# TensorE held to the program's order while a token mixing runs, side steps behind whole units of big products

## The chip, the cores and the metric

One core of a Trainium2 chip runs the whole kernel. The metric is device time in microseconds (us) of one launch; the kernel before takes 1155.15 us, the median of 3 runs (1153.23 to 1157.84).

## The reference, cut to what matters

One layer on 528 tokens (16 meta tokens and 512 frames) of width 1024:

```
h += 0.5 * swiglu(rmsnorm(h))                    # FFN 1, inner width 2816
z  = rmsnorm(h) @ w_in                           # 2464 columns
h += concat(rwkv7(z[:, :1696]), attention(z[:, 1696:])) @ w_out
h += 0.5 * swiglu(rmsnorm(h))                    # FFN 2
out = rmsnorm(h)[16:]
# rwkv7: 8 heads of 64, a recurrence over the tokens
#   S = S*w_t + (S @ -kk_t) (kk_t*a_t)^T + v_t k_t^T ;  y_t = S r_t
# attention: 8 query and 2 key heads, chunks of 64 frames, a window of 3 chunks,
#   the meta tokens and a sink
```

## The kernel before

Tokens run along the free axis in two halves: half 0 has 272 (16 meta tokens and 256 frames), half 1 has 256. A *unit* is one 128-column tile of a weight matrix with 8 blocks of 128 rows: `prep` loads 512 KB through SyncE's queue (L120), ScalarE casts them to the high half `whi` (L122), VectorE subtracts to get the low half `wlo` (L125), and TensorE does 24 matmuls of 128 x 272 or 128 x 256 (high by high, high by low, low by high: L199, L200, L195, and L208 in the down projections). `raw`, `whi` and `wlo` have three buffers each, and units are prepared three ahead. A unit's accumulator (tile `big`, four PSUM banks) is then evicted by VectorE and ScalarE.

`drive` (L131) traces the units of a list in order; after each it calls `advance` (L166), which gives every running side chain the unit's cost as credit (2.72 for half 0, 2.56 for half 1). A side chain is a Python generator: it traces one step, yields what the step costs, and is called again while its credit is positive. The list (L1032 to L1040): four units of half 1's FFN 1; the 14 units of half 0's input projection that feed RWKV, with elementwise work and small matmuls behind each (`on_z`; the last small matmul of each of four head pairs is L561); `begin`, which starts the RWKV chain; the 6 units of attention's projection; `begin_at`, which starts the attention chain; the other 62 units of half 1's FFN 1; `end`, which joins the chains; 8 units of output projection (`w_out`). Then the same for half 1's mixing, with 6 + 56 units of half 0's FFN 2 as cover.

The RWKV chain: `tinv` sends gram tiles through DRAM (L681 and L685, on ScalarE's queue), VectorE inverts 80 triangular 32 x 32 blocks in 31 dependent pairs of operations (L694, L696; phase `tik`), the result goes back through DRAM (L702 to L714), and 64 + 64 matmuls of 32 x 32 finish it (L721, L729; phase `tizo`). `chain` then goes through 5 chunks (4 in half 1), each in steps: X and Z (L781, L784), the solve (L796), values of the next chunk (L759, L764), state and output (L806 to L816), and a group norm with one matmul (L840). These matmuls write the tile `mx`, two PSUM banks. Attention goes through 4 chunks, each a transposition of V (L868), and twice: scores (L878), softmax, transposition (L898), product (L910).

The trace order isn't the order on the chip: at compile time a scheduler models the engines and puts on each the instruction that is ready first, the earlier traced first among those; `high_priority` moves the RWKV steps ahead (100 for `chain`, 0 for `tik`). So big products traced later can stand ahead of a small matmul that waits for its data.

Of the kernel before, what the change touches and what calls it, by code (L numbers as in the profile page):

```python
# [32 lines left out]
BRIDGE = 4  # L33
WO = (4, 5, 6, 7, 0, 1, 2, 3)
WARM = 12
TIW, CHW, ATW = 1.4, 0.55, 0.9
NK = D // 128


# [26 lines left out]
NU = len(UNIT)  # L66


class Prog:
    def __init__(self, ctx, tc, io):  # L70
        self.tc, self.nc, self.io = tc, tc.nc, io
        self.A, self.V, self.P, self.PE = tc.nc.scalar, tc.nc.vector, tc.nc.gpsimd, tc.nc.tensor
        self.uid = 0
        pool = lambda name, **k: ctx.enter_context(tc.tile_pool(name=name, bufs=1, **k))
        self.cst = pool("cst")
        self.rp = pool("res")
        self.np_ = pool("npl")
# [88 lines left out]
    def advance(self, cost):  # L166
        for sd in list(self.sides):
            if sd not in self.sides:
                continue
            sd[1] += cost  # L170
            while sd[1] > 0:
                self.mark(self.ph or sd[2] if sd[2] == 'rwkv' else sd[2])
                with self.tc.high_priority(PRIO.get(self.ph if sd[2] == "rwkv" else "", PRIO[sd[2]])):
                    c = next(sd[0], None)
                if c is None:
                    self.sides.remove(sd)
                    break
                sd[1] -= c

# [492 lines left out]
    def tinv(self, hf, mp, tip):  # L672
# [40 lines left out]
            nc.scalar.dma_start(out=T1c[hr[h]].rearrange("s p c t -> s (p c) t"), in_=d3[g].rearrange("g s t -> s g t"))  # L713
            nc.scalar.dma_start(out=T2c[hr[h]].rearrange("s p c t -> s (p c) t"), in_=d2[1, g].rearrange("g s t -> s g t"))  # L714
        self.ph = 'tizo'
        yield 6.0
        pc = [(p, c, slice((p * 4 + c - 1) * 32, (p * 4 + c) * 32)) for p in range(4) for c in range(1, 5)]
        bz = self.mbank()
        for p, c, o in pc:
# [2 lines left out]
        Z = t(tip, [128, 512], "Z")  # L722
        for h in range(2):
            (A.copy, V.tensor_copy)[h](out=Z[hr[h]], in_=bz[hr[h]])
        yield 2.0
        bo = self.mbank()
        for p, c, o in pc:
            for h in range(2):
# [1 line left out]
        for h in range(2):  # L730
            (A.copy, V.tensor_copy)[h](out=GT[hr[h], 4 * h:4 * h + 4, 1:5, 32:64],
                                       in_=bo[hr[h]].rearrange("p (h s t) -> p h s t", h=4, s=4))
        yield 2.0

    def chain(self, hf, st, mo, cp):

# [32 lines left out]
            pre[n] = (UV, BT)  # L769

        values(0)
        yield CHW
        hp = [(p, h) for p in range(4) for h in range(2)]
        for n, (slot, tok, C) in enumerate(chunks):
            self.ph = f'ch{slot}'
            ur, vr = (slice(0, C), slice(64, 64 + C)), (slice(64, 64 + C), slice(0, C))
            gt = lambda rows, h, p, c: GT[rows[h], 4 * h + p, slot, c:c + C]
            UV, BT = pre.pop(n)
            X, Z = self.mbank(), self.mbank() if slot else None
            for p, h in hp:  # L780
                PE.matmul(X[ur[h], cols(p)], gt(vr, h, p, 0), UV[vr[h], h, p], start=True, stop=True)  # L781
            if slot:
                for p, h in hp:
                    PE.matmul(Z[hs[h], cols(p)], self.AR[p][hs[h], slot, 0:64], S[hs[h], p], start=True, stop=True)  # L784
            Rs = t(cp, [128, 256], "Rs")
            if slot:
                A.copy(out=Rs, in_=X[:, 0:256])
                V.tensor_tensor(out=Rs, in0=Z[:, 0:256], in1=Rs, op=ALU.add)
            else:
                for h in range(2):  # L790
                    A.copy(out=Rs[ur[h]], in_=X[ur[h], 0:256])
            step()
            yield 2 * CHW
            X = self.mbank()
            for p, h in hp:
                PE.matmul(X[ur[h], cols(p)], gt(ur, h, p, 0), Rs[ur[h], cols(p)], start=True, stop=True)  # L796
            for h in range(2):
                (A.copy, V.tensor_copy)[h](out=UV[ur[h], h], in_=X[ur[h], 0:256].rearrange("p (j c) -> p j c", j=4))
            step()
            yield CHW  # L800
            if n + 1 < len(chunks):
                values(n + 1)
            yield CHW
            X, Z = self.mbank(), self.mbank()
            for p, h in hp:
                PE.matmul(Z[hs[h], cols(p)], BT[vr[h], h, p], UV[vr[h], h, p], start=True, stop=True)  # L806
                PE.matmul(X[hs[h], cols(p)], BT[ur[h], h, p], UV[ur[h], h, p], start=True, stop=True)
            if slot:
                for p in range(4):
                    for h in range(2):  # L810
                        PE.matmul(X[hs[h], cols(p, 256)], S[hs[h], p], self.AR[p][hs[h], slot, 64:64 + C],
                                  start=True, stop=False)
                    for h in range(2):
                        PE.matmul(Z[hs[h], cols(p, 256)], UV[vr[h], h, p], gt(vr, h, p, 64), start=True, stop=True)
                    for h in range(2):
                        PE.matmul(X[hs[h], cols(p, 256)], UV[ur[h], h, p], gt(ur, h, p, 64), start=False, stop=True)  # L816
            p4 = lambda b, c: b[:, c:c + 256].rearrange("p (j c) -> p j c", j=4)
            for b in (Z, X):
                V.tensor_tensor(out=S, in0=p4(b, 0), in1=S, op=ALU.add)
            V.tensor_tensor(out=S, in0=S, in1=st["ee"][:, :, slot].unsqueeze(2).broadcast_to([128, 4, 64]), op=ALU.mult)  # L820
            if slot:
                Y = t(cp, [128, 4, 64], "Y", bufs=2)
                A.copy(out=Y, in_=p4(Z, 256))
                V.tensor_tensor(out=Y, in0=p4(X, 256), in1=Y, op=ALU.add)
                norms.append(self.group_norm(st, mo, cp, Y, slice(64 * slot - 64, 64 * slot)))
            step()
            yield 2 * CHW
        self.ph = 'gn'
        while norms:
            step()  # L830
            yield 2.0

    def group_norm(self, st, mo, cp, Y, ts):

# [18 lines left out]
    def attention(self, hf, st, mo, ap_):  # L853
        A, V, P, PE, t = self.A, self.V, self.P, self.PE, self.t
        for ci in range(4):
# [14 lines left out]
                PE.transpose(b[0:W - 81, 128:256], VC[:, 81:W], self.ident)  # L870
                A.copy(out=VK[0:W - 81, 1], in_=b[0:W - 81, 128:256])
            A.copy(out=VK[0:81, 0], in_=b[0:81, 0:128])
            yield ATW
            kss = (slice(0, 64), slice(64, 128))
            for mp2 in range(2):
                bs, rows = self.banks(), []
# [3 lines left out]
                for kv in range(2):  # L880
# [6 lines left out]
                                           scalar=-3e38, op0=ALU.add, op1=ALU.max, accum_out=m[:, 1:2])  # L887
                    V.tensor_scalar(out=m[:, 2:3], in0=m[:, 0:1], scalar1=m[:, 1:2], scalar2=-1.0, op0=ALU.max, op1=ALU.mult)
                    rows.append((s, m))
                yield ATW  # L890
                for s, m in rows:
                    A.activation(s[:, 0:W], s[:, 0:W], AF.Exp, bias=m[:, 2:3], accum_out=m[:, 3:4])
                yield ATW
                b, bo = self.banks()
                for kv, (s, m) in enumerate(rows):
                    V.reciprocal(m[:, 3:4], m[:, 3:4])
                    A.activation(s[:, 0:W], s[:, 0:W], AF.Copy, scale=m[:, 3:4])
                    PE.transpose(b[0:81, 256 * kv:256 * kv + 128], s[:, 0:81], self.ident)  # L898
                    if nw > 1:
                        PE.transpose(b[0:W - 81, 256 * kv + 128:256 * kv + 256], s[:, 81:W], self.ident)  # L900
                yield ATW
                pTs = []
                for kv in range(2):
                    pT = t(ap_, [128, 2, 128], "pT", bufs=2)
# [6 lines left out]
                if nw > 1:  # L911
                    for kv, ks in enumerate(kss):
                        PE.matmul(bo[ks, 0:128], VK[0:W - 81, 1, ks], pTs[kv][0:W - 81, 1], start=False, stop=True)
                yield ATW
                ms, ts = slice(2 * mp2, 2 * mp2 + 2), slice(64 * ci, 64 * ci + 64)
                ov = bo[:, 0:128].rearrange("p (m t) -> p m t", m=2)
                mh, ml = mo[1][:, ms, 0, ts], mo[1][:, ms, 1, ts]
                A.copy(out=mh, in_=ov)
                V.tensor_tensor(out=ml, in0=ov, in1=mh.bitcast(F32), op=ALU.subtract)
                yield ATW  # L920


def program(tc, io, out):
    with ExitStack() as ctx:
# [37 lines left out]
        def pclose(name):  # L962
            pools.pop(name)[0].__exit__(None, None, None)
# [11 lines left out]
        def mixing(hf):  # L975
            st, mo = {}, []

            def on_z():
                return pr.on_z(hf, st, pools["mix"][1], pools["ew"][1] if "ew" in pools else None)

            def begin_ew():
                popen("ew")

            def rwkv():
                yield from pr.tinv(hf, pools["mix"][1], popen("ti"))
                pclose("ti")
                cp = popen("ch")
                yield from pr.chain(hf, st, mo, cp)
                pclose("ch")

            def begin():
                pclose("ew")
                popen("at")
                mo.extend(pr.operands(hf, 256))
                pr.side(rwkv(), "rwkv")

            def begin_at():
                pr.side(pr.attention(hf, st, mo, pools["at"][1]), "attn")

            def end():  # L1000
                pr.join()
                pclose("at")
            return on_z, act(begin_ew), act(begin), act(begin_at), act(end), mo

# [32 lines left out]
        k = 10  # L1037
# [131 lines left out]
```

## Time and profile before

| | before |
|---|---|
| median of 3 runs | 1155.15 us |
| the profiled execution | 1155.86 us |
| its span, first to last instruction | 1154.0 us |
| TensorE busy | 1113.4 us (96%), 10149 matmuls |
| VectorE busy | 801.7 us (69%) |
| ScalarE busy | 661.8 us (57%) |
| mean granted TensorE clock | 0.976 |

The rows quoted below are from that one execution. An engine is busy while it executes an instruction; a matmul's end is modelled, so TensorE counts as busy also where matmuls follow each other at half the clock. The profile names engines PE (TensorE), DVE (VectorE), ACT (ScalarE), POOL (GpSimd), SP (SyncE); L12 is line 12.

### The profile page before, as it was taken

How to read it: one execution, taken by the hardware profiler on the slowest of the kernel's cores; microseconds unless marked ns; L12 is line 12 of the kernel's file. 1: busy time of each engine (PE TensorE's matmuls, PEld its weight loads, DVE VectorE, ACT ScalarE, POOL GpSimd, SP SyncE). 2: the span in 40 equal slices, each digit the busy share in tenths (PEclk: the TensorE clock that was granted, in tenths of full speed). 3: DMA queues.
4: the chain of work that ended last, by engine and by line, in shares of the span. 5: the costliest groups of instructions: out<-in, count | busy, mean ns of one | idle time of the engine just before them, and what ended most of it. 6: DMA issues, size and time to landing. Idle time of an engine off the chain costs nothing.

```text
span 1154.0 us, 24751 instructions
## 1 busy us (share of the span) xinstructions
PE 1113.4 (96%) x10149; PEld 1065.9 (92%) x10149; DVE 801.7 (69%) x1465; ACT 661.8 (57%) x1118; POOL 37.3 (3%) x91
## 2 busy tenths in 40 slices
PE   8999999999999998999899999997999899999996
PEld 7999999998999997899899898987889899999996
DVE  7866566776778993356888777995356686655555
ACT  7544444686757646565568685574456476444343
POOL 0000000021000000000001000000000000000000
PEclk8999999999999999899999999998899899999998
DMA  7565555545445555223255345456223456665662
GB/s 270 173 184 184 189 175 177 171 133 160 129 130 186 163 169 148 74 95 114 92 184 177 128 142 174 149 163 168 75 82 121 117 166 203 199 207 182 187 185 74
DMA packets 68724, 178.87 MB, mean 155 GB/s; under 512 B 21620, under 2 KB 26868, under 8 KB 68612
## 3 DMA queue, kind: packets, MB, share of 16 engines
q1 hardware_dynamic: 52384, 173.70, 47.9%
q10 hardware_dynamic: 16228, 3.61, 1.5%
q8 instruction: 79, 1.29, 0.5%
q14 instruction: 33, 0.27, 0.1%
HBM read 173.54 MB, written 3.74 MB: 154 GB/s over the span
## 4 chain that ended last, share of the span: by engine, by line
PE 79%; DVE 11%; ACT 3%; DMA 3%; issue 2%; ACTq 1%; DVEq 0%; SPq 0%
PE big L200 23%; PE big L199 23%; PE big L195 16%; PE big L208 6%; DVE wlo L125 4%; DVE tmp L694 3%; DVE rn L696 2%; PE mx L764 1%; ACT whi L122 1%; PE mx L759 1%; DMA raw<-w_in 1%; DMA d<-rn 1%; PE as L878 1%; PE mx L806 1%; PE mx L796 1%
## 5 line engine op out<-in xcount | busy, mean ns | idle before, releaser
L122 ACT CAST whi<-raw 128x1024 fp32r<-128x1024 f32 (+1 forms) x321 | 334.9, 1045 | 283.3 <-PE big L200 205.5
L125 DVE TENSOR_TENSOR wlo<-raw,whi 128x1024 fp32r<-128x1024 f32 x320 | 389.5, 1218 | 105.6 <-ACT whi L122 82.7
L200 PE MATMUL big<-h,whi 128*128 128x256 f32 (+1 forms) x704 | 177.0, 286 | 0.0
L199 PE MATMUL big<-h,whi 128*128 128x256 f32 (+1 forms) x704 | 173.2, 285 | 0.0
L200 PEld LDWEIGHTS big<-h,whi 128*128 128x128 f32 x704 | 133.1, 190 | 1.5 <-issue 0.9
L199 PEld LDWEIGHTS big<-h,whi 128*128 128x128 f32 x704 | 132.3, 190 | 0.6 <-issue 0.3
L199 PE MATMUL big<-n1a,whi 128*128 128x256 f32 x464 | 121.0, 292 | 8.9 <-ACT n1a L849 4.2
L199 PE MATMUL big<-n0a,whi 128*128 128x272 f32 (+1 forms) x464 | 122.3, 293 | 6.4 <-ACT n0a L849 3.2
L200 PE MATMUL big<-n0a,whi 128*128 128x272 f32 (+1 forms) x464 | 121.5, 290 | 0.6 <-DVE n0a L328 0.6
L199 PE MATMUL big<-n0b,whi 128*128 128x272 f32 (+1 forms) x464 | 120.7, 291 | 0.7 <-ACT n0b L327 0.7
L200 PE MATMUL big<-n0b,whi 128*128 128x272 f32 (+1 forms) x464 | 120.1, 288 | 0.4 <-DVE n0b L328 0.4
L200 PE MATMUL big<-n1b,whi 128*128 128x256 f32 x464 | 119.9, 289 | 0.0
L200 PE MATMUL big<-n1a,whi 128*128 128x256 f32 x464 | 119.8, 288 | 0.0
L199 PE MATMUL big<-n1b,whi 128*128 128x256 f32 x464 | 119.3, 288 | 0.0
L208 PE MATMUL big<-h,wlo 128*128 128x256 f32 (+1 forms) x704 | 106.1, 286 | 0.0
L199 PEld LDWEIGHTS big<-n1a,whi 128*128 128x128 f32 x464 | 90.5, 195 | 11.6 <-ACT n1a L849 4.6
L199 PEld LDWEIGHTS big<-n0a,whi 128*128 128x128 f32 x464 | 88.2, 191 | 9.0 <-ACT n0a L849 3.4
L208 PEld LDWEIGHTS big<-h,wlo 128*128 128x128 f32 x704 | 93.8, 190 | 1.1 <-issue 0.6
L200 PEld LDWEIGHTS big<-n1a,whi 128*128 128x128 f32 x464 | 90.5, 195 | 0.7 <-issue 0.3
L200 PEld LDWEIGHTS big<-n1b,whi 128*128 128x128 f32 x464 | 90.0, 194 | 1.2 <-issue 0.2
L199 PEld LDWEIGHTS big<-n1b,whi 128*128 128x128 f32 x464 | 89.8, 194 | 1.3 <-issue 0.8
L200 PEld LDWEIGHTS big<-n0a,whi 128*128 128x128 f32 x464 | 88.4, 191 | 2.5 <-DVE n0a L328 1.0
(294 smaller groups left out, 2032.2 us busy)
## 6 DMA issues: line engine op xcount, KB each, us to landing
raw<-w_in SPq DMA_DIRECT2D x319, 512.0 KB, 3.7
outT<-o SPq DMA_DIRECT2D x8, 256.0 KB, 2.2
res<-xT_in SPq DMA_DIRECT2D x2, 544.0 KB, 4.3
res<-xT_in SPq DMA_DIRECT2D x2, 512.0 KB, 8.6
d<-GT ACTq DMA_DIRECT2D x8, 80.0 KB, 3.6
zk<-d ACTq DMA_DIRECT2D x2, 320.0 KB, 5.1
d<-rn ACTq DMA_DIRECT2D x2, 320.0 KB, 3.6
GT<-d ACTq DMA_DIRECT2D x8, 80.0 KB, 5.8
```

The lines of the kernel that those rows point to most:

```text
L122: self.A.copy(out=hi[:, a:a + n], in_=raw[:, a:a + n])
L125: self.V.tensor_tensor(out=lo[:, 0:nk], in0=raw[:, 0:nk], in1=hi[:, 0:nk].bitcast(F32), op=ALU.subtract)
L195: self.PE.matmul(o, lo[:, k], x(k)[:, 0], start=False, stop=(k == ks[-1]))
L199: self.PE.matmul(o, w, x[:, 0], start=first, stop=False)
L200: self.PE.matmul(o, w, x[:, 1], start=False, stop=False)
L208: self.PE.matmul(o, lo[:, i], x(k)[:, 0], start=False, stop=(k == nk - 1))
L694: V.tensor_tensor(out=m, in0=NT[:n2, 0:k, k].unsqueeze(1).broadcast_to([n2, k, k]), in1=TI[:n2, 0:k, 0:k], op=ALU.mult)
L696: V.tensor_reduce(out=TI[:n2, 0:k, k], in_=m, op=ALU.add, axis=mybir.AxisListType.X)
L759: PE.matmul(b[vr[h], cols(p)], st["vT", p][hs[h], tok:tok + C], self.cent[hs[h], hs[h]], start=True, stop=True)
L764: PE.matmul(b[hs[r], cols(p, 256)], self.BK[p][hs[h], slot, hs[r ^ h]], self.ident[hs[h], hs[h]], start=True, stop=True)
L796: PE.matmul(X[ur[h], cols(p)], gt(ur, h, p, 0), Rs[ur[h], cols(p)], start=True, stop=True)
L806: PE.matmul(Z[hs[h], cols(p)], BT[vr[h], h, p], UV[vr[h], h, p], start=True, stop=True)
```

## The change

The chains no longer yield costs (but for `tik`, whose yields stay): they yield `UNIT_END`, at which `advance` sets their credit to zero and stops, so that one step of each chain is traced behind each whole unit. TensorE is wrapped (`Pinned`); from `begin` to `end` each matmul and transposition gets an order edge to the instruction traced before it on TensorE, which the scheduler must keep. The wait of 6.0 ahead of `tizo` becomes four empty steps. X and Z are traced alternately, `values` comes into the same step as the solve, attention's reciprocal and scaling move up to the exponential, with one empty step behind them. No matmul is added or removed, and no DMA.

```diff
@@ -33,7 +33,9 @@
 BRIDGE = 4
 WO = (4, 5, 6, 7, 0, 1, 2, 3)
 WARM = 12
-TIW, CHW, ATW = 1.4, 0.55, 0.9
+TIW = 1.4
+
+UNIT_END = -1.0
 NK = D // 128
 
 
@@ -66,10 +68,28 @@
 NU = len(UNIT)
 
 
+class Pinned:
+
+
+    def __init__(self, tc, pe):
+        self.tc, self.pe, self.on = tc, pe, False
+
+    def matmul(self, *a, **k):
+        return self.pin(self.pe.matmul(*a, **k))
+
+    def transpose(self, *a, **k):
+        return self.pin(self.pe.transpose(*a, **k))
+
+    def pin(self, ins):
+        if self.on:
+            self.tc.keep_in_program_order(ins)
+        return ins
+
+
 class Prog:
     def __init__(self, ctx, tc, io):
         self.tc, self.nc, self.io = tc, tc.nc, io
-        self.A, self.V, self.P, self.PE = tc.nc.scalar, tc.nc.vector, tc.nc.gpsimd, tc.nc.tensor
+        self.A, self.V, self.P, self.PE = tc.nc.scalar, tc.nc.vector, tc.nc.gpsimd, Pinned(tc, tc.nc.tensor)
         self.uid = 0
         pool = lambda name, **k: ctx.enter_context(tc.tile_pool(name=name, bufs=1, **k))
         self.cst = pool("cst")
@@ -174,6 +194,9 @@
                     c = next(sd[0], None)
                 if c is None:
                     self.sides.remove(sd)
+                    break
+                if c == UNIT_END:
+                    sd[1] = 0.0
                     break
                 sd[1] -= c
 
@@ -713,7 +736,8 @@
             nc.scalar.dma_start(out=T1c[hr[h]].rearrange("s p c t -> s (p c) t"), in_=d3[g].rearrange("g s t -> s g t"))
             nc.scalar.dma_start(out=T2c[hr[h]].rearrange("s p c t -> s (p c) t"), in_=d2[1, g].rearrange("g s t -> s g t"))
         self.ph = 'tizo'
-        yield 6.0
+        for _ in range(4):
+            yield UNIT_END
         pc = [(p, c, slice((p * 4 + c - 1) * 32, (p * 4 + c) * 32)) for p in range(4) for c in range(1, 5)]
         bz = self.mbank()
         for p, c, o in pc:
@@ -779,8 +803,7 @@
             X, Z = self.mbank(), self.mbank() if slot else None
             for p, h in hp:
                 PE.matmul(X[ur[h], cols(p)], gt(vr, h, p, 0), UV[vr[h], h, p], start=True, stop=True)
-            if slot:
-                for p, h in hp:
+                if slot:
                     PE.matmul(Z[hs[h], cols(p)], self.AR[p][hs[h], slot, 0:64], S[hs[h], p], start=True, stop=True)
             Rs = t(cp, [128, 256], "Rs")
             if slot:
@@ -790,17 +813,16 @@
                 for h in range(2):
                     A.copy(out=Rs[ur[h]], in_=X[ur[h], 0:256])
             step()
-            yield 2 * CHW
+            yield UNIT_END
             X = self.mbank()
             for p, h in hp:
                 PE.matmul(X[ur[h], cols(p)], gt(ur, h, p, 0), Rs[ur[h], cols(p)], start=True, stop=True)
             for h in range(2):
                 (A.copy, V.tensor_copy)[h](out=UV[ur[h], h], in_=X[ur[h], 0:256].rearrange("p (j c) -> p j c", j=4))
-            step()
-            yield CHW
             if n + 1 < len(chunks):
                 values(n + 1)
-            yield CHW
+            step()
+            yield UNIT_END
             X, Z = self.mbank(), self.mbank()
             for p, h in hp:
                 PE.matmul(Z[hs[h], cols(p)], BT[vr[h], h, p], UV[vr[h], h, p], start=True, stop=True)
@@ -824,11 +846,11 @@
                 V.tensor_tensor(out=Y, in0=p4(X, 256), in1=Y, op=ALU.add)
                 norms.append(self.group_norm(st, mo, cp, Y, slice(64 * slot - 64, 64 * slot)))
             step()
-            yield 2 * CHW
+            yield UNIT_END
         self.ph = 'gn'
         while norms:
             step()
-            yield 2.0
+            yield UNIT_END
 
     def group_norm(self, st, mo, cp, Y, ts):
 
@@ -887,18 +909,19 @@
                                            scalar=-3e38, op0=ALU.add, op1=ALU.max, accum_out=m[:, 1:2])
                     V.tensor_scalar(out=m[:, 2:3], in0=m[:, 0:1], scalar1=m[:, 1:2], scalar2=-1.0, op0=ALU.max, op1=ALU.mult)
                     rows.append((s, m))
-                yield ATW
                 for s, m in rows:
                     A.activation(s[:, 0:W], s[:, 0:W], AF.Exp, bias=m[:, 2:3], accum_out=m[:, 3:4])
-                yield ATW
+                for s, m in rows:
+                    V.reciprocal(m[:, 3:4], m[:, 3:4])
+                    A.activation(s[:, 0:W], s[:, 0:W], AF.Copy, scale=m[:, 3:4])
+                yield UNIT_END
+                yield UNIT_END
                 b, bo = self.banks()
                 for kv, (s, m) in enumerate(rows):
-                    V.reciprocal(m[:, 3:4], m[:, 3:4])
-                    A.activation(s[:, 0:W], s[:, 0:W], AF.Copy, scale=m[:, 3:4])
                     PE.transpose(b[0:81, 256 * kv:256 * kv + 128], s[:, 0:81], self.ident)
                     if nw > 1:
                         PE.transpose(b[0:W - 81, 256 * kv + 128:256 * kv + 256], s[:, 81:W], self.ident)
-                yield ATW
+                yield UNIT_END
                 pTs = []
                 for kv in range(2):
                     pT = t(ap_, [128, 2, 128], "pT", bufs=2)
@@ -993,12 +1016,14 @@
                 popen("at")
                 mo.extend(pr.operands(hf, 256))
                 pr.side(rwkv(), "rwkv")
+                pr.PE.on = True
 
             def begin_at():
                 pr.side(pr.attention(hf, st, mo, pools["at"][1]), "attn")
 
             def end():
                 pr.join()
+                pr.PE.on = False
                 pclose("at")
             return on_z, act(begin_ew), act(begin), act(begin_at), act(end), mo
 
```

The hunks left out replace the yields of `tizo`, of `values(0)` and of attention's other steps by `UNIT_END`.

## Rows read from the trace of the kernel before

**Rows 1.** The page, part 1: busy us (share), instructions of each engine.

```profile
PE 1113.4 (96%) x10149; PEld 1065.9 (92%) x10149; DVE 801.7 (69%) x1465; ACT 661.8 (57%) x1118; POOL 37.3 (3%) x91
```

**Rows 2.** The page, part 4: the chain that ended last, by engine.

```profile
PE 79%; DVE 11%; ACT 3%; DMA 3%; issue 2%; ACTq 1%; DVEq 0%; SPq 0%
```

**Rows 3.** Windows: span, then busy us (x instructions) PE, PEld, DVE, ACT, POOL, clock, DMA.

```profile
1008.00:1032.00 24.00, 24.00 (x205) 24.00 (x205) 13.74 (x18) 10.32 (x12) 0.00 (x0) 1.00 0.61 200
```

**Rows 4.** Windows by stage of the two mixings, columns as above.

```profile
273.50:340.30 66.80, 65.19 (x561) 59.31 (x560) 47.20 (x102) 41.56 (x70) 3.83 (x15) 1.00 0.41 120
340.30:442.10 101.80, 98.45 (x820) 94.30 (x818) 89.14 (x193) 58.27 (x107) 0.90 (x4) 1.00 0.59 173
442.10:559.50 117.40, 116.73 (x1516) 105.21 (x1516) 65.25 (x139) 70.89 (x144) 0.00 (x0) 0.94 0.32 105
633.60:692.50 58.90, 57.85 (x527) 52.85 (x525) 44.31 (x77) 41.58 (x72) 2.09 (x8) 1.00 0.44 139
692.50:793.10 100.60, 96.02 (x804) 91.96 (x801) 87.10 (x185) 57.65 (x108) 9.30 (x14) 1.00 0.57 170
793.10:897.70 104.60, 99.45 (x1315) 89.33 (x1316) 56.22 (x122) 58.84 (x125) 0.48 (x2) 0.92 0.33 98
```

**Rows 5.** Windows, instructions on tile big alone: PE, PEld, DVE, ACT, clock, DMA.

```profile
273.50:340.30 66.80, 52.67 (x397) 48.98 (x395) 3.16 (x7) 5.14 (x13) 1.00 0.41 120
340.30:442.10 101.80, 92.73 (x737) 88.94 (x735) 9.80 (x24) 3.07 (x8) 1.00 0.59 173
442.10:559.50 117.40, 74.49 (x508) 67.29 (x507) 6.75 (x16) 3.10 (x8) 0.94 0.32 105
633.60:692.50 58.90, 48.08 (x374) 45.03 (x372) 3.08 (x7) 5.17 (x12) 1.00 0.44 139
692.50:793.10 100.60, 90.52 (x725) 86.69 (x725) 7.49 (x18) 3.43 (x9) 1.00 0.57 170
```

**Rows 6.** L561 in the two projections: ns min/median/max, first and last start.

```profile
L561 PE MATMUL mx<-zr,bones x4: 377/378/379, 304.0 to 340.5; 128*128 128x256 f32 x4
L561 PE MATMUL mx<-zr,bones x4: 379/431/484, 659.5 to 692.9; 128*128 128x256 f32 x4
```

**Rows 7.** VectorE's groups, 288 to 343: busy us, mean ns, idle before.

```profile
L125 DVE TENSOR_TENSOR wlo<-raw,whi 128x1024 fp32r<-128x1024 f32 x14 | 17.1, 1221 | 5.3 <-ACT whi L122 4.2 <-PE big L195 0.7 <-PE big L208 0.3
```

**Rows 8.** VectorE's groups, 342 to 430.

```profile
L125 DVE TENSOR_TENSOR wlo<-raw,whi 128x1024 fp32r<-128x1024 f32 x28 | 33.9, 1211 | 1.4 <-ACT whi L122 1.4
L694 DVE TENSOR_TENSOR tmp<-zk,rn 80x1 f32<-80x1 f32 (+30 forms) x31 | 24.0, 773 | 3.2 <-DMA zk<-d 2.9
L696 DVE TENSOR_REDUCE rn<-tmp 80x1 f32<-80x1 f32 (+30 forms) x31 | 15.4, 495 | 0.3
```

**Rows 9.** VectorE in order of time: start, us, operation, idle before.

```profile
352.29 0.15 DVE L694 TENSOR_TENSOR tmp<-zk,rn 80x1 f32<-80x1 f32 x1 [2.90 <-DMA zk<-d]
```

**Rows 10.** The chain of waits, 426 to 443: start, us, what.

```profile
428.43 3.66 DMA d<-rn
```

**Rows 11.** L721 in the two mixings: first and last start at the end.

```profile
L721 PE MATMUL mx<-zk,GT x42: 190/192/213, 442.1 to 445.6; 32*32 32x32 f32 x42
L721 PE MATMUL mx<-zk,GT x64: 190/236/258, 793.1 to 802.4; 32*32 32x32 f32 x64
```

**Rows 12.** TensorE in order of time, two chunks of the chain.

```profile
508.13 0.51 PE L784 MATMUL mx<-S,AR 64*64 64x64 f32 x11
510.71 0.59 PE L840 MATMUL mx<-gsq,bones 128*128 128x256 f32 x2
...
526.27 0.51 PE L781 MATMUL mx<-UV,GT 64*64 64x64 f32 x10
```

**Rows 13.** TensorE in order of time, at the output projection's start.

```profile
563.01 0.28 PE L200 MATMUL big<-n0b,whi 128*128 128x256 f32 x1
566.50 1.01 PE L199 MATMUL big<-n0a,whi 128*128 128x256 f32 x3 [3.21 <-ACT n0a L849]
...
568.06 0.41 PE L200 MATMUL big<-n0a,whi 128*128 128x256 f32 x1
```

More of the change, by code (lines that the diff above doesn't have):

```diff
@@ L732, in tinv @@
                                        in_=bo[hr[h]].rearrange("p (h s t) -> p h s t", h=4, s=4))
-        yield 2.0
+        yield UNIT_END
     def chain(self, hf, st, mo, cp):
@@ L798, in chain @@
                 (A.copy, V.tensor_copy)[h](out=UV[ur[h], h], in_=X[ur[h], 0:256].rearrange("p (j c) -> p j c", j=4))
-            step()
-            yield CHW
             if n + 1 < len(chunks):
                 values(n + 1)
-            yield CHW
+            step()
+            yield UNIT_END
             X, Z = self.mbank(), self.mbank()
@@ L830, in chain @@
             step()
-            yield 2.0
+            yield UNIT_END
     def group_norm(self, st, mo, cp, Y, ts):
@@ L872, in attention @@
             A.copy(out=VK[0:81, 0], in_=b[0:81, 0:128])
-            yield ATW
+            yield UNIT_END
             kss = (slice(0, 64), slice(64, 128))
@@ L889, in attention @@
                     rows.append((s, m))
-                yield ATW
                 for s, m in rows:
                     A.activation(s[:, 0:W], s[:, 0:W], AF.Exp, bias=m[:, 2:3], accum_out=m[:, 3:4])
-                yield ATW
+                for s, m in rows:
+                    V.reciprocal(m[:, 3:4], m[:, 3:4])
+                    A.activation(s[:, 0:W], s[:, 0:W], AF.Copy, scale=m[:, 3:4])
+                yield UNIT_END
+                yield UNIT_END
                 b, bo = self.banks()
                 for kv, (s, m) in enumerate(rows):
-                    V.reciprocal(m[:, 3:4], m[:, 3:4])
-                    A.activation(s[:, 0:W], s[:, 0:W], AF.Copy, scale=m[:, 3:4])
                     PE.transpose(b[0:81, 256 * kv:256 * kv + 128], s[:, 0:81], self.ident)
@@ L900, in attention @@
                         PE.transpose(b[0:W - 81, 256 * kv + 128:256 * kv + 256], s[:, 81:W], self.ident)
-                yield ATW
+                yield UNIT_END
                 pTs = []
@@ L913, in attention @@
                         PE.matmul(bo[ks, 0:128], VK[0:W - 81, 1, ks], pTs[kv][0:W - 81, 1], start=False, stop=True)
-                yield ATW
+                yield UNIT_END
                 ms, ts = slice(2 * mp2, 2 * mp2 + 2), slice(64 * ci, 64 * ci + 64)
@@ L919, in attention @@
                 V.tensor_tensor(out=ml, in0=ov, in1=mh.bitcast(F32), op=ALU.subtract)
-                yield ATW
+                yield UNIT_END
 def program(tc, io, out):
```

## The prediction

> **What bounds the kernel now.** First the busy shares: TensorE is busy 96% of the span and VectorE 69% [rows 1]. Then the chain that ended last: 79% of it is TensorE, 11% VectorE [rows 2]. So the time is the length of TensorE's stream, and a change pays by taking idle time or overhead out of it, or costs by putting some in. The length of a unit (24 big matmuls, one weight tile) comes from a stretch with nothing else in it: 205 matmuls in 24.0 us, so 2.81 us with 256 columns [rows 3]; I take 2.85, and 2.95 for the 272 columns of half 0.
>
> Next the table by stage, in which the reader should compare VectorE with TensorE. Half 0's mixing has three stretches [rows 4]: from the end of 14 units' worth of input projection (273.5) to the last L561 (340.3), the last TensorE work traced ahead of the mixing; from there to the first tizo matmul L721 (442.1); and from there to the end of the FFN that covers it (559.5). In the second VectorE is busy 89.1 of 101.8 us: that stretch belongs to VectorE, and TensorE stays busy only because the scheduler lets big products through. How many, the table of the accumulator tile shows [rows 5]: 397 and 737 matmuls, 16.5 and 30.7 units, so 47 units pass between the projection and L721. Half 1 has 374 and 725, which is 15.6 and 30.2 units.
>
> **What the change removes.** Once `begin` has run, each matmul follows the one traced before it. The first pinned one belongs to input projection 14, and it follows L561 of the fourth head pair. So the 16.5 (15.6) units that run ahead of L561 today can't. And how many units may stand between L561 and L721 is now the trace's: tik costs 6 credits plus twice the sum of (k*k/960 + 0.08) times 1.4 over 31 steps, 37.3, together 43.3 at 2.72 (six units) and 2.56 credits a unit, so tik's last step is traced behind unit 17; four empty steps follow, and L721 stands behind unit 21. Where 47 and 46 units cover the way to L721, 21 will. The mixing then ends in time: the chain's 15 steps (12 in half 1), norms and tizo reach to unit 42 (39), attention's 44 steps from unit 7 to 50, of 68 (62) units.
>
> **Wait one: L561.** TensorE will stand before unit 14 until the fourth pair's elementwise work is done; queued behind it are all big products, and behind these the SiLU evictions, the release of weight buffers to ScalarE's and VectorE's casts, and SyncE's weight loads. When will L561 come? Today the last ones run at 340.5 and 692.9 [rows 6]. At the latest, there again. At the earliest, when VectorE does this work with no gap: 47.2 us busy in the stretch [rows 4], less 17.1 for 14 low halves that won't be made [rows 7], is 30 us, so 303.5; half 1 likewise, 655. I take 26 us off: the 17.1, and half as much again for their casts and the FFN's evictions on the same two engines. That gives 314 and 667. From 273.5 TensorE has some 7 us of small matmuls, so it idles about 34 us; from 633.6, about 26.
>
> **Wait two: L721.** Behind L561 TensorE has six units at 2.95, fifteen at 2.85 and some 4 us of attention: 65 us. The data take longer. Today the way is 101.6 us (340.5 to 442.1) and 100.2 us [rows 6, 11]. In it lie 39.4 us of tik on VectorE [rows 8], 11.8 us from L561 to tik's first operation [rows 6, 9], and the DMA round trips behind tik: the first leaves at 428.43, L721 starts at 442.1, 13.7 us [rows 10, 11], issued by ScalarE between its casts as today. VectorE also makes 28 low halves, 33.9 us [rows 8]; with 21 units in the stretch it makes 21, and evicts less: 7 times 1.7 us less, 12. So 90 us by that sum; I take 93 and 91, because the first 11.8 us can't take all of the rest. Lower end: nothing but 11.8, 39.4 and 13.7, which is 65, no wait at all; upper end today's 101.6. L721 thus starts at 407 and 758, after some 27 us of waiting each time.
>
> **Behind L721.** Left are 68 less 21 units, 47 at 2.85: 134 us; half 1, 41: 117 us. The small matmuls: in 117.4 us today 508 of 1516 matmuls are big, 60 us, so the other 1008 and all that is lost beside them cost 57 us, at a mean clock of 0.94 [rows 4, 5]. Without the clock's share (7) and with fewer switches between kinds (4, estimated; bounds 0 and 10) I take 46, for half 1, which has one chunk less, 42. New here: a step's second part waits in TensorE's queue. L840 takes a bank that the step just before it filled: today it starts 2.1 us behind that step's last matmuls (508.1 plus 0.5, to 510.7), while big products run [rows 12]; pinned right behind them it holds the queue, four times a mixing, and L759 in the same way behind L796. For this and for steps whose copies need more than one unit I take 15 and 13 us; bounds 0 and 25. Gained: today the big products run out before the norms and TensorE idles 3.2 us at 566.5 [rows 13]; then the mixing will be long over.
>
> **The sum.** Half 0: 407 + 134 + 46 + 15 = 602, against 566.5 less 2 us of output projection done ahead: +37. Half 1: 758 + 117 + 42 + 13 = 930, against 897.7 plus the like wait of 3 us: +29. For the clock behind the four waits I add 1.2 us each, +5 (bounds 0 and 10): behind the 3.2 us wait a big matmul shows 0.41 us, ahead of it 0.28 [rows 13]. Together +71. The profiled execution took 1155.9 us (span 1154.0), 0.7 above the median of 1155.15: 1156 + 71 = 1227, taken as 1226 against the median. The regrouping of X and Z matmuls, the earlier reciprocal and the two empty attention steps change no count and lie beside VectorE and ScalarE time that is free behind L721 (65.3 and 70.9 of 117.4 us [rows 4]); uncovered, they would cost what the steps' wait term already bounds.
>
> The Trainium skill (PSUM — Partial Sum Buffer, Engine vs sequencer instructions) says that matmuls start and complete in program order. By that rule nothing on the engine itself softens these waits, and a wait of the one matmul is a wait of all behind it; no run here shows it otherwise.
>
> **The rivals.** (a) Faster. Relieved of other units' casts, VectorE and ScalarE rush: L561 at the lower ends, L721 65 us behind it, no chain waits. Half 0 ends at 303.5 + 65 + 134 + 46 = 548, -16; half 1 at 655 + 64 + 117 + 42 = 878, -23: 1117. For it: fewer switches, a steadier clock (0.94 and 0.92 in the third stretches [rows 4]). Against: it needs VectorE's 25 us of low halves to vanish into the gaps before tik and behind it, 25 us, in which big products' evictions also run. It decides from a distance L561 to L721 of about 75 us downward. The Trainium skill (TensorEngine Tiling (Array Packing), Key Properties) adds that a change of tiling mode drains the engine, which speaks for whole units; here that is inside the switch term and worth at most the 10 us given. (b) No change within 0.5%: the pin doesn't hold, big products pass as before: 1156. Against: every big and small matmul goes through the pinned wrapper. (c) Only wait two comes, since L561 keeps up: 60 us less, 1166. (d) Worse: the chain's steps wait nearly every unit, as the 18 us from one chunk's first matmuls (to 508.6) to the next one's (526.3) suggest [rows 12], where three units and a chunk's small matmuls would be some 15 us, and dense runs of small matmuls halve the clock: 25 to 30 us more in each mixing (18 us a chunk through, and the clock), 1286; were L721 no earlier than today besides, 1317.
>
> **How the numbers follow.** Forecast 0.62 (1195 to 1260); (a) 0.09; (b) 0.05; (c) 0.10; (d) 0.14. A measurement of this kernel can tell about 0.5% from no change. Faster is (a), 0.09; same is (b), 0.05; the rest, 0.86, slower. The range 1162 to 1288 takes in the forecast, (c) and half of (d).
>
> **What would show it.** Right: two TensorE gaps of over 15 us in each mixing, the first ended by L561, the second by the DMA or L699's tile in front of L721; 21 units between them; VectorE's tik shorter than today; third stretches with 47 and 41 units. Wrong: TensorE busy through either place, L561 still near 340 with big products ahead of it, or L721 less than 75 us behind L561. If the stretch behind L721 is over 215 us long in half 0, rival (d) has the step waits right.

## The result, and the profile after

The changed kernel takes 1233.9 us (median of 4 runs, 1230.05 to 1239.98), the kernel before 1154.5 us beside it: a ratio of 1.068, with an interval of 1.0655 to 1.0705. The forecast was 1226 and slower. The profiled execution of the changed kernel took 1230.05 us, which is 74.2 more than the one of before.

The page first: busy us of each engine (share, instructions), TensorE's busy tenths and its granted clock in 40 slices.

```profile
span 1228.3 us, 24746 instructions
...
PE 1101.9 (90%) x10149; PEld 1056.0 (86%) x10149; DVE 806.9 (66%) x1465; ACT 663.0 (54%) x1117; POOL 39.3 (3%) x91
...
PE   8999999996896687999999579768799999999996
...
PEclk8999999995799798999999679979899999999999
```

Against [rows 1] the matmuls are as many and TensorE is busy 11.5 us less, in a span that is 74.3 longer. Its idle time, span less busy, went from 40.6 to 126.4 us: +85.8. So the whole loss is idle time, and more than the loss. The two dents in the busy line lie in the two mixings.

Windows, stage by stage: span, then busy us (x instructions) of PE, PEld, DVE, ACT, POOL, clock, DMA share, GB/s. The four of half 0 run from the end of the projection to the last L561 matmul, to the last big product ahead of `tizo`, to the first `tizo` matmul (L721 in the kernel before), and to the output projection; then the four of half 1, the third of which still holds the last of its 21 units. The profile gives every matmul of the changed kernel the wrapper's line L78 (transpositions L81), so tiles, not lines, tell them apart.

```profile
273.70:316.70 43.00, 26.75 (x168) 18.47 (x167) 28.28 (x79) 14.56 (x34) 3.47 (x15) 0.53 0.06 18
316.70:390.90 74.20, 70.67 (x549) 67.60 (x547) 63.52 (x128) 36.94 (x63) 2.74 (x4) 0.95 0.45 137
390.90:407.00 16.10, 0.00 (x0) 0.00 (x0) 8.84 (x15) 5.62 (x10) 0.00 (x0) 0.66 0.61 159
407.00:607.50 200.50, 180.71 (x2177) 171.10 (x2178) 106.86 (x215) 113.84 (x213) 0.10 (x1) 0.95 0.39 120
680.30:721.50 41.20, 20.39 (x153) 12.79 (x151) 24.70 (x55) 13.88 (x34) 2.37 (x8) 0.57 0.05 18
721.50:790.00 68.50, 64.10 (x525) 61.53 (x524) 62.55 (x128) 40.90 (x72) 8.42 (x10) 0.98 0.51 150
790.00:806.30 16.30, 2.75 (x25) 2.55 (x23) 9.74 (x13) 6.05 (x12) 0.00 (x0) 0.67 0.57 153
806.30:976.30 170.00, 156.65 (x1921) 148.11 (x1922) 93.36 (x192) 98.10 (x185) 1.58 (x6) 0.95 0.41 123
```

The same, instructions on the tile `big` alone, half 0's second and fourth stretch.

```profile
316.70:390.90 74.20, 66.68 (x504) 64.13 (x504) 4.20 (x10) 4.70 (x12) 0.95 0.45 137
...
407.00:607.50 200.50, 147.30 (x1129) 142.23 (x1130) 13.13 (x31) 5.75 (x15) 0.95 0.39 120
```

Where 397 and 737 big products stood ahead of and beside the inversion [rows 5], there are none in the first stretch (2 of 168 matmuls by the same view) and 504, exactly 21 units, in the second; 1129, that is 47 units, are left for behind `tizo`, and they run over a stretch that was 117.4 us long [rows 4] and is now 200.5.

TensorE in order of time, half 0: start, us, what, count, and in brackets the idle time before it with what ended it.

```profile
278.53 0.90 PE L78 MATMUL mx<-AR,BK 64*64 64x128 f32 x3 [4.25 <-DVE BK L661]
...
289.87 0.66 PE L78 MATMUL as<-AR,BK 64*64 64x128 f32 x2 [3.04 <-DVE BK L661]
...
302.06 0.90 PE L78 MATMUL mx<-AR,BK 64*64 64x128 f32 x3 [3.90 <-DVE BK L661]
...
407.06 0.31 PE L78 MATMUL mx<-zk,GT 32*32 32x32 f32 x2 [16.18 <-DMA zk<-d]
...
458.92 0.70 PE L78 MATMUL mx<-gsq,bones 128*128 128x256 f32 x2 [0.60 <-ACT Rs L810]
...
468.21 0.79 PE L78 MATMUL mx<-cent,vT 64*64 64x64 f32 x9 [4.35 <-DVE UV L821]
```

All of TensorE's larger waits by tile and releaser: us in total, times, the longest.

```profile
PE mx L78 <- DMA zk<-d: 31.5, 4, 16.2
PE mx L78 <- DVE UV L821: 19.3, 7, 4.4
PE mx L78 <- DVE BK L661: 17.1, 4, 4.7
PE as L78 <- DVE BK L661: 11.0, 4, 3.0
PE as L81 <- ACT s L916: 7.3, 5, 3.0
PE mx L78 <- ACT Rs L810: 6.9, 6, 2.1
```

These six are 93 of the 126.4 us. Three kinds are new: the elementwise work of the head pairs ahead of L561 (`BK`), the inversion's result coming back through DRAM (`zk<-d`), and copies inside a chain step (`UV` and `Rs`), each with every later matmul standing behind it. The wait for attention's softmax (`s`) isn't: it took 9.5 us in the kernel before.

### The profile page after: what moved, and what is told of

Its sections match the earlier page's. It is cut to its first block, busy times and chain, and to the rows that moved or that the text cites. A ratio compares the mean times of both kernels' runs of the same rounds, so it can differ in the third digit from the quotient of the medians.

```text
span 1228.3 us, 24746 instructions
## 1 busy us (share of the span) xinstructions
PE 1101.9 (90%) x10149; PEld 1056.0 (86%) x10149; DVE 806.9 (66%) x1465; ACT 663.0 (54%) x1117; POOL 39.3 (3%) x91
## 5 line engine op out<-in xcount | busy, mean ns | idle before, releaser
L78 PE MATMUL big<-h,whi 128*128 128x256 f32 (+1 forms) x1408 | 192.3, 286 | 3.3 <-DVE h L396 1.9
L78 PEld LDWEIGHTS big<-h,whi 128*128 128x128 f32 x1408 | 178.7, 191 | 6.3 <-DVE h L396 2.5
L78 PE MATMUL big<-n0a,whi 128*128 128x272 f32 (+1 forms) x928 | 141.6, 295 | 3.3 <-ACT n0a L350 1.8
L78 PE MATMUL big<-n0b,whi 128*128 128x272 f32 (+1 forms) x928 | 137.2, 290 | 1.0 <-ACT n0b L350 0.6
L78 PE MATMUL big<-n1a,whi 128*128 128x256 f32 x928 | 137.4, 291 | 0.0
L78 PE MATMUL big<-n1b,whi 128*128 128x256 f32 x928 | 133.2, 287 | 0.0
L78 PEld LDWEIGHTS big<-n0a,whi 128*128 128x128 f32 x928 | 125.2, 194 | 8.2 <-issue 2.3
L78 PEld LDWEIGHTS big<-n0b,whi 128*128 128x128 f32 x928 | 124.2, 192 | 2.8 <-ACT n0b L350 1.1
L78 PEld LDWEIGHTS big<-n1a,whi 128*128 128x128 f32 x928 | 122.9, 196 | 3.0 <-issue 1.8
L78 PEld LDWEIGHTS big<-n1b,whi 128*128 128x128 f32 x928 | 122.6, 196 | 0.1
L78 PE MATMUL big<-h,wlo 128*128 128x256 f32 (+1 forms) x704 | 101.9, 282 | 0.0
L78 PEld LDWEIGHTS big<-h,wlo 128*128 128x128 f32 x704 | 91.8, 188 | 0.0
L78 PE MATMUL big<-n1a,wlo 128*128 128x256 f32 x464 | 76.2, 286 | 0.0
L78 PE MATMUL big<-n0a,wlo 128*128 128x272 f32 (+1 forms) x464 | 75.4, 285 | 0.0
L78 PE MATMUL big<-n0b,wlo 128*128 128x272 f32 (+1 forms) x464 | 75.3, 284 | 0.0
L78 PE MATMUL big<-n1b,wlo 128*128 128x256 f32 x464 | 74.5, 283 | 0.0
L78 PEld LDWEIGHTS big<-n1a,wlo 128*128 128x128 f32 x464 | 65.4, 196 | 0.1
L78 PEld LDWEIGHTS big<-n0a,wlo 128*128 128x128 f32 x464 | 64.5, 190 | 0.0
```

Source lines behind the costliest of these rows:

```text
L78: return self.pin(self.pe.matmul(*a, **k))
```

## The experiments

**The order alone against the rest of the change.** `e1_no_pin` keeps all of the change but the switch that turns the order edges on.

```diff
                 pr.side(rwkv(), "rwkv")
-                pr.PE.on = True
```

> The change without its order edges: TensorE's order is again the scheduler's, the steps are still traced one behind each unit. Theory (the two waits come from the pinned order): big products pass L561 and tizo again, no TensorE gap over 5 us ahead of tizo, 1140 to 1170 us. Rival (the pacing itself, one step behind each unit, stretches the mixing): 1200 us or more, with the mixings ending as late as in the changed kernel.

Measured: 1140.6 us, ratio 0.986 (0.983 to 0.989). Its page and two windows, in the second and (half 1) third stretch; last, the same end of half 1's mixing in the kernel before:

```profile
PE 1100.2 (97%) x10149; PEld 1059.5 (93%) x10149; DVE 802.1 (70%) x1465; ACT 662.3 (58%) x1120; POOL 37.0 (3%) x91
...
340.60:440.10 99.50, 96.80 (x812) 93.09 (x810) 88.07 (x191) 55.23 (x102) 0.91 (x4) 1.00 0.61 177
...
791.00:888.00 97.00, 92.34 (x1324) 84.99 (x1324) 60.14 (x136) 61.36 (x130) 0.51 (x2) 0.96 0.36 107
...
791.00:902.50 111.50, 101.43 (x1330) 90.71 (x1328) 59.27 (x127) 59.92 (x127) 0.48 (x2) 0.92 0.33 96
```

So the order costs 93 us, and the rest of the change gains some 14. Span 1138.9 less 1100.2 busy is 38.7 us of idle time against 126.4: without the edges the idle time is back at what it was before. The stretch up to `tizo` is within 2.3 us of before [rows 4]; the gain lies behind it, most of it in half 1, where the way from 791 to the output projection takes 97.0 us with 1324 matmuls and took 111.5 with 1330. Busy time is the same with and without the edges (1100.2 and 1101.9 us) though the mean granted clock is 0.979 and 0.935.

**Are the waits two costs, or one?** `e3_pin_later` turns the order on only at `begin_at`, six units later, so that those units may pass L561.

```diff
                 pr.side(rwkv(), "rwkv")
-                pr.PE.on = True
 
             def begin_at():
+                pr.PE.on = True
```

> The pin begins behind attention's six projection units, so that big products may pass L561 again; tizo still stands behind unit 21. Theory (not TensorE's wait at L561 but the path L561, inversion, tizo sets the time): TensorE is busy through the place of wait one, L561 moves from 316 back to about 335, tizo's first matmul stays at 405 to 420 behind a TensorE wait of 40 us or more, and the time stays within 1220 to 1250. Rival (the waits add up, as the sum had it): wait one's idle is saved whole, 55 us, 1170 to 1190.

Measured: 1233.9 us, ratio 1.068 (1.066 to 1.069), the same as the whole change. Windows from the projection to `tizo`, and the first `tizo` matmul:

```profile
273.50:329.30 55.80, 44.63 (x352) 36.76 (x350) 37.79 (x89) 28.25 (x54) 4.76 (x19) 0.82 0.28 83
329.30:382.00 52.70, 49.43 (x362) 47.26 (x363) 42.72 (x114) 24.21 (x48) 0.00 (x0) 0.90 0.42 130
382.00:407.50 25.50, 0.34 (x3) 0.13 (x2) 18.98 (x18) 2.79 (x5) 0.00 (x0) 0.55 0.34 80
...
407.56 0.31 PE L78 MATMUL mx<-zk,GT 32*32 32x32 f32 x2 [25.22 <-DMA zk<-d]
```

With TensorE busy 44.6 instead of 26.8 us in the first stretch, `tizo` starts at 407.6 as it did at 407.1: what isn't idled away at the first place is idled away at the second (25.2 us, where 16.2 had been; less than the 40 that I had expected, and L561 starts last at 326, not 335). The first wait is smaller, not gone: by waits, `BK` has 16.0 us where it had 28.1, `zk<-d` 51.0 where it had 31.5. What stays constant is VectorE. From the projection to `tizo` it is busy 99.5 us here (37.8 + 42.7 + 19.0) and 100.6 in the changed kernel (28.3 + 63.5 + 8.8), in 134.0 and 133.3 us. In the kernel before it was 136.3 (47.2 + 89.1) in 168.6 [rows 4]. VectorE's own idle time on that way is 32 to 35 us in all three (in half 1, 28.1 us before and 29.0 in the changed kernel). So wherever TensorE waits for `tizo`, its date is VectorE's work in the window plus some 30 us; the next run cuts that work.

**Does the inversion's way set `tizo`?** `e4_tik_cut` leaves out the last ten of the inversion's 31 pairs of operations, 23.4 us of VectorE in each mixing, and keeps their credits.

```diff
         for k in range(1, 32):
+            if k >= 22:
+                yield 2 * (k * k / 960.0 + 0.08) * TIW
+                continue
```

> The last ten of the inversion's 31 pairs of VectorE operations (k from 22, 23.4 us of VectorE in each mixing) are left out; all else, order and pin too, stays. Theory (wait two is VectorE's inversion being late, not the DMA round trip): the TensorE idle ahead of tizo goes (16.2 and 13.6 us), and no more than that, 1200 to 1210 us. Rival (the DMA trips and ScalarE's queue hold tizo): idle ahead of tizo falls by under 5 us, 1225 or more.

Measured: 1196.5 us, ratio 1.036 (1.033 to 1.039). Its page, and the first `tizo` matmul:

```profile
PE 1101.5 (92%) x10149; PEld 1056.2 (88%) x10149; DVE 766.0 (64%) x1425; ACT 660.0 (55%) x1115; POOL 35.4 (3%) x91
...
391.50 1.20 PE L78 MATMUL mx<-zk,GT 32*32 32x32 f32 x64
```

The wait is gone, and `tizo` starts right behind its 21 units, 15.6 us earlier. Between the profiled executions the span went from 1228.3 to 1195.2, 33.1 us; the row `zk<-d` was 31.5. So with less work on VectorE this wait goes, and it cost about its own length. (The medians differ by 37, which puts the time below the 1200 to 1210 that I expected; the profiled execution of the changed kernel was the fastest of its four.) Not all of the way is VectorE's: in the changed kernel the inversion's last operation ends at 398.7, and `tizo` starts some 8 us later, behind the DMA trips, which no run shortened.

```profile
397.58 1.13 DVE L719 TENSOR_REDUCE rn<-tmp 80x31 f32<-80x961 f32 x1
```

**Can more units fill the second wait?** `e2_ten_empty` has ten empty steps where there were four, so 27 units stand ahead of `tizo`.

```diff
         self.ph = 'tizo'
-        for _ in range(4):
+        for _ in range(10):
             yield UNIT_END
```

> Ten empty steps ahead of tizo in place of four, pin kept: six more units, 17 us, may stand ahead of tizo's first matmul in each mixing. Theory: the idle ahead of it (16.2 and 13.6 us in the changed kernel) is filled, tizo starts no later than 2 us after it does now, and the time falls by 25 to 32 us to 1202 to 1209. Rival (a wait filled there comes back, since the casts of six more units delay the inversion, or the chain then ends too late): 1225 or more.

Measured: 1210.2 us, ratio 1.047 (1.045 to 1.049). The inversion's last operation, the first `tizo` matmul, and a row of the waits:

```profile
394.76 1.18 DVE L719 TENSOR_REDUCE rn<-tmp 80x31 f32<-80x961 f32 x1
...
419.09 1.07 PE L78 MATMUL mx<-zk,GT 32*32 32x32 f32 x56
...
PE as L81 <- ACT s L916: 23.9, 8, 6.6
```

The wait is gone here too, but `tizo` comes 12 us later, not within 2 as I expected. The rival's reason for that, an inversion delayed by six more units' casts, isn't what the trace shows: the inversion ends at 395.9, 2.8 us earlier than in the changed kernel, and its last transfers to `zk` are issued at 402.7. This time TensorE is late: it has six more units ahead of `tizo`, some 17 us, and waits 8.2 us there for attention's softmax, whose small VectorE operations stand among the inversion's. So ten steps are more than the wait could hold. They brought 24 us, less than the 31.5 of the wait, since attention's transpositions now wait 23.9 us in all where they waited 7.3; and 1210 is just outside what I expected.

**Do the waits inside a step cost what I gave them?** `e8_values_own` puts the values of the next chunk into a step of their own, one unit behind the solve whose copies they need.

```diff
+            step()
+            yield UNIT_END
             if n + 1 < len(chunks):
                 values(n + 1)
-            step()
             yield UNIT_END
```

> The changed kernel with the next chunk's values (L759, L764 of before) in a step of their own, behind a whole unit, instead of right behind the solve; the pin stays. Theory (these matmuls hold the queue while ScalarE and VectorE empty the bank that the solve filled: 11.3 us idle in the first mixing, 8.0 in the second): that idle goes, 1208 to 1222 us. Rival (the same copies then hold the next step): 1228 or more.

Measured: 1204.7 us, ratio 1.043 (1.039 to 1.0465). Its page, the first `tizo` matmul and the waits:

```profile
PE 1097.9 (91%) x10149; PEld 1053.2 (87%) x10149; DVE 806.6 (67%) x1465; ACT 662.2 (55%) x1117; POOL 36.7 (3%) x91
...
406.35 0.31 PE L78 MATMUL mx<-zk,GT 32*32 32x32 f32 x2 [15.99 <-DMA zk<-d]
...
PE mx L78 <- DMA zk<-d: 31.0, 4, 16.0
PE mx L78 <- ACT Rs L810: 6.1, 6, 1.7
```

`tizo` stays, the row `UV` is gone, and the span falls by 24.5 us (1228.3 to 1203.8): 20.5 of idle time, of which the row was 19.3, and 4.0 of busy time. So these waits cost at least what they show; the medians differ by 29, below the 1208 that I had as the lower end.

**All covers at once.** `e7_cover_all` keeps the order but traces 16 (half 1: 12) FFN units ahead of `begin`, behind the projection, and has 12 empty steps ahead of `tizo`.

```diff
-        for _ in range(4):
+        for _ in range(12):
...
-        steps += fb[:BRIDGE] + wa[0] + wa[1] + ma[2] + wa[2] + ma[3]
-        steps += fb[BRIDGE:] + ma[4] + pr.w_out(0, ma[5], renorm("f2", 2))
+        steps += fb[:BRIDGE] + wa[0] + wa[1] + fb[BRIDGE:BRIDGE + 16] + ma[2] + wa[2] + ma[3]
+        steps += fb[BRIDGE + 16:] + ma[4] + pr.w_out(0, ma[5], renorm("f2", 2))
...
-        steps += wb[0] + wb[1] + mb[2] + wb[2] + mb[3]
+        steps += wb[0] + wb[1] + fa[:12] + mb[2] + wb[2] + mb[3]
...
-        steps += fa[:-k] + mb[4] + act(lambda: pclose("mix"))
+        steps += fa[12:-k] + mb[4] + act(lambda: pclose("mix"))
```

> Pin kept, but the trace gives TensorE nearly the units that the kernel before passes ahead of tizo: 16 units of the covering FFN (12 in the second mixing) are traced between the RWKV projection and the pin's beginning, and twelve empty steps stand ahead of tizo, so 45 (41) units where the changed kernel has 29 with the eight added empty steps alone and 21 in itself. Theory (the loss is the trace position under a pin, not the pin as such): no TensorE idle over 5 us at L561 or tizo, what is left of the loss is the step waits of some 15 us a mixing, 1150 to 1172 us. Rival (holding the program's order costs wherever the units stand): 1190 or more.

Measured: 1163.2 us (10 runs), ratio 1.0073 (1.005 to 1.0095). Its three largest waits:

```profile
PE as L81 <- ACT s L916: 26.2, 9, 9.8
PE mx L78 <- DVE UV L821: 13.8, 7, 2.9
PE big L78 <- ACT silu L393: 6.9, 3, 2.8
```

No row for `BK` or `zk<-d` is among them. 71 of the 79 us come back with the order kept: most of the loss was that units which had covered VectorE's part came to stand behind it. Against `e1_no_pin` the order, with the units at these places, still costs 23 us: 77.8 us idle against 38.7, but 1086.4 busy against 1100.2. The waits of attention's steps, 26.2 us, have taken the others' place.

**Where does the gain without the order come from?** `e9_regroup` is the kernel before with X and Z in turn, the values in the solve's step and attention's scaling moved up, and the old credits.

```diff
-            if slot:
-                for p, h in hp:
+                if slot:
                     PE.matmul(Z[hs[h], cols(p)], ...
...
-            step()
-            yield CHW
             if n + 1 < len(chunks):
                 values(n + 1)
-            yield CHW
+            step()
+            yield 2 * CHW
...
+                for s, m in rows:
+                    V.reciprocal(m[:, 3:4], m[:, 3:4])
+                    A.activation(s[:, 0:W], s[:, 0:W], AF.Copy, scale=m[:, 3:4])
...
-                    V.reciprocal(m[:, 3:4], m[:, 3:4])
-                    A.activation(s[:, 0:W], s[:, 0:W], AF.Copy, scale=m[:, 3:4])
```

> The kernel before, its credits kept and no order edge, with the change's regrouping alone: X and Z matmuls in turn, values traced with the solve, attention's exponential and scaling moved ahead. Theory (the gain of the change without its pin, 15 us, is the pacing, one step behind each unit): no change, 1148 to 1160 us. Rival (the regrouping brings that gain): 1145 or less.

Measured: 1154.4 us (10 runs), ratio 0.999 (0.996 to 1.001): no change. By elimination the gain of `e1_no_pin` would belong to what is left, one step behind each unit instead of costs and credits; that pacing wasn't tried alone.

`e10_no_pin_values_own` is `e1_no_pin` with the edit of `e8_values_own`.

```diff
-                pr.PE.on = True
...
+            step()
+            yield UNIT_END
             if n + 1 < len(chunks):
                 values(n + 1)
-            step()
             yield UNIT_END
```

> No order edges, the pacing kept, values in a step of their own. Without the pin big products fill the place where the pinned queue stood, so the theory expects no more than a few us against the pacing alone (1140.6): 1134 to 1146. Rival (values ahead of a whole unit shorten the chain's path): under 1134.

Measured: 1132.65 us, ratio 0.9815 (0.979 to 0.984), the fastest of all, and 1.4 us under the 1134 at which the rival begins. Its page, and windows behind `tizo` in half 0 and half 1:

```profile
PE 1087.1 (96%) x10149; PEld 1047.1 (93%) x10149; DVE 801.7 (71%) x1465; ACT 660.0 (58%) x1119; POOL 39.3 (3%) x91
...
440.00:560.00 120.00, 114.66 (x1574) 105.52 (x1573) 75.19 (x155) 76.40 (x158) 0.10 (x1) 0.99 0.35 107
...
791.00:880.00 89.00, 85.17 (x1245) 78.73 (x1244) 55.54 (x123) 55.39 (x119) 0.51 (x2) 1.00 0.33 107
```

Idle time is that of the kernel before (41.7 and 40.6 us); what fell is busy time, by 26.3 us [rows 1], above all in the stretches behind `tizo`: a matmul there takes 73 and 68 ns (114.66 by 1574, 85.17 by 1245) at a clock of 0.99 and 1.00, in the kernel before 77 and 76 ns at 0.94 and 0.92 [rows 4]. All four runs (1130.9 to 1134.5) lie below those of `e1_no_pin` (1136.1 to 1142.9), but the two intervals, each against its own runs of the kernel before, touch (0.984 and 0.983): that the values' own step adds something is likely, how much isn't settled. Against `e1_no_pin` idle time doesn't fall (38.7 and 41.7 us), busy time does, by 13.1, so the rival's reason, a shorter path of the chain, isn't shown either.

## Why the prediction was right, and which terms were off

**Right: what sets the time, and the date of `tizo`.** 21 units stand between L561 and `tizo`, and 47 behind it, as counted from the credits. L561 was put at 314 and starts last at 316.7; `tizo` at 407 and started at 407.06; the output projection at 602, and started at 607.5 (41 us behind the 566.5 of before; on the sum's base, 564.5, it is 43 where it had 37). In half 1 the same three were put at 667, 758 and 930; less the 41 us by which half 0's end came late they are 680.4, 765 and 935: L561 13 us later than put, the other two 7 and 5. The lateness of the two halves, 41 and then 78.6 in all (976.3 against 897.7), less 4.4 us that came back behind, is the 74.2 of the profiled executions; the sum said 71.

**Right in the sum, not in the reason given.** The two waits were summed up as if each were a cost. `e3_pin_later` shows that they hang together: both come out of VectorE's work up to `tizo`. I had taken 26 us off ahead of L561 and 9 behind, together 35. VectorE's busy time fell by 18.9 and 16.8 (47.2 to 28.3, 89.1 to 72.4), together 35.7, and the way by 35.2 (168.6 to 133.4). In half 0 the dates moved much as put (23.8 and 11.2 us), in half 1 by 12.5 and 15.3: that the split came out in half 0 is partly luck. Rival (c), with L561 keeping up for 1166, has `e3_pin_later` against it: with less of the first wait the second grows.

**The sign was met in part.** I had named two gaps of over 15 us in each mixing, the first of them ended by L561. Ahead of L561 there is no such gap. I had TensorE stop once, before unit 14; it stops several times, at each head pair's small matmuls, for up to 4.25 us in half 0 and 4.7 in half 1. And half 1's second gap is 13.6 us.

**Mis-sized, without moving `tizo`: how the idle time divides.** I gave the first wait 34 us and 7 us of small matmuls; the stretch shows 16.3 us idle and 26.8 busy. For the same matmuls (166 without the tile `big`; 561 less 397, 164 before) TensorE was busy 12.5 us before (65.2 less 52.7; my 7 was too low already by those rows) [rows 4, 5], and is busy 26.6 now. The L561 matmuls show why, one view by tile of the changed kernel (ns of one, min/median/max, first and last start):

```profile
L78 PE MATMUL mx<-zr,bones x4: 634/714/793, 292.9 to 316.7; 128*128 128x256 f32 x4
```

They took 377 to 379 ns [rows 6]. The mean granted clock of the stretch is 0.53, about the lower of its two levels (1.2 of 2.4 GHz); what TensorE did there is small matmuls between waits of 1 to 4 us. The Trainium skill (TensorE: Matmul & The Clock Gate, Part 1: The HAM clock gate (the "warmup" mystery)) says that the default state is throttled and activity releases it; the trace agrees: 0.53 here, 0.95 in the next stretch, where big products follow each other. What of it reached `tizo` isn't shown apart; little, by `e3_pin_later`, where the first stretch has 0.82 and `tizo` the same date. The second wait, put at 27 us, was 16.2 (half 1: 13.6 of 16.3), because the 21 units took 74.2 us instead of 65; again the date didn't move.

**Mis-sized, cancelling: the step waits and their owner.** 15 and 13 us were given; the rows show 26.2 us (`UV` 19.3, `Rs` 6.9). But I named L840 first, four times 2.1 us, and the values in passing. Measured, L840 with `Rs` costs 0.5 to 2.1 us, six times, and the values behind the solve up to 4.4 us, seven times. `e8_values_own` takes just that away. The step that failed is the reading of [rows 12]: they show L840's distance in today's order, and nothing of the values, which the change itself put into the solve's step. I had weighed that regrouping as hidden or inside the waits' term; it is most of that term.

**Right in size, at fewer places: the clock.** 1.2 us were added for each of four waits, +5. Behind the second wait the trace shows it: the granted clock is 0.50 from 408 to 412 and 1.00 from 414. First the changed kernel, then `e4_tik_cut`, which has no wait there:

```profile
410.89 2.05 PE L78 MATMUL big<-n1a,whi 128*128 128x256 f32 x8
...
393.05 1.19 PE L78 MATMUL big<-n1a,whi 128*128 128x256 f32 x8
```

From the first `tizo` matmul to the next 64 (on `t2c`, at 414.95) it is 7.9 us, 0.9 of it a wait; in `e4_tik_cut` (391.50 to 396.08) 4.6. So the clock costs some 2.4 us there, and as much in half 1 (8.0 us, 0.9 a wait): twice the size given, at half the places. The totals don't settle it: `e4_tik_cut` gained 1.6 us beyond the 31.5 of the wait, but its stretch behind `tizo`, at 0.92 instead of 0.95, took 202.3 us instead of 200.5.

**Not seen: what the rest is worth.** The regrouping was taken to cost nothing uncovered and the steadier stream behind `tizo` to save 11 us in each mixing (57 to 46). `e1_no_pin` shows 13.2 us less busy time than before and 14 us less in all, as a gain of its own that the order hides. The Trainium skill (TensorEngine Tiling (Array Packing), Key Properties) has a change of tiling mode drain the engine; what that is worth, which I held to be at most those 10 us, can't be told apart here from the clock's part, which rose with it.

**The other rivals.** (a) needed `tizo` within 75 us of L561; it was 90.4. (b) fell with 21 units in the second stretch. (d) needed over 215 us behind `tizo`; it was 200.5, at a clock of 0.95, not half. Two prices don't follow from my rows, and the forecast uses neither: half 1's earliest L561 is 633.6 + 44.3 - 17.1 = 661, not 655, which makes (a) 1123; and `tizo` at today's dates (442.1 and 793.1 for 407 and 758) would add some 70 us to (d), not 31. The Trainium skill (PSUM — Partial Sum Buffer, Engine vs sequencer instructions) has matmuls start and complete in program order; the trace agrees: in front of `tizo` not one matmul runs in 16.1 us, though VectorE's last cast for the big products behind it in the order ends at 397.6.

## What to carry to other kernels

Before holding an engine to an order, add up the work of the other engine that must be done by each pinned date, and count the units that the order leaves to cover it (too few and it waits there, too many and the pinned step comes late, as with ten empty steps): here 47 units covered VectorE's way, the order left 21, and some 60 of the 86 us of added idle time (31.5, 17.1 and 11.0) follow from that. The waits that such an order shows at several places may be one deadline; move one of them, and see whether the sum changes. And a pinned step should hold no copy that its own second part waits for: put the part that needs the copy one unit later.

## What was unexpected of the hardware

Of TensorE's clock: waits of no more than 4.3 us, with small matmuls between them, went with a mean of 0.53 over 43 us, and the same matmuls took 634 to 793 ns instead of 378. And behind `tizo`, with TensorE busy 95% and more, the clock still differs with the order of big and small matmuls: 0.94 and 0.92 in the kernel before [rows 4], 0.99 and 1.00 in `e10_no_pin_values_own`, which has the same 10149 matmuls and 26.3 us less busy time. What of that is the clock and what the changes between kinds of matmul stays open; how many there are of these wasn't counted.
